# Rotary embedding on one core: 32 KB rows instead of 16 KB, and a ring of five 4 MB tiles instead of ten 2 MB ones

## The chip, the core and the metric

The kernel runs on one core of a Trainium2 chip. A core has five engines that run their own instruction streams: TensorE (PE in the profile), VectorE (DVE), ScalarE (ACT), GpSimd (POOL) and SyncE (SP), and 16 DMA engines that move data between DRAM and the on-chip memory SBUF (128 partitions). TensorE writes its results to a second memory, PSUM. Engines wait for one another, and for transfers, on semaphores. [...]the DMA engines then work through its packets. The metric is the device time of one execution in microseconds, the median of five runs.

## What is computed

The input x is 16 batches x 512 positions x 1024 float32, and each row of 1024 is 16 heads of 64 numbers. Each head's two halves are rotated by the angle of the position (the table index is the position; all heads and all batches share it):

```
x = x.reshape(batch, seq, num_heads, head_dim)
x1, x2 = x[..., :half_dim], x[..., half_dim:]
cos = cos[None, :, None, :]        # 512 x 32
sin = sin[None, :, None, :]
out = concatenate([x1 * cos - x2 * sin, x1 * sin + x2 * cos], axis=-1)
```

33.55 MB are read and 33.55 MB are written.

## The kernel before

One batch (512 rows, 2 MB) is one transfer, `c` in the code. Its 512 rows lie on 128 partitions with R = 4 neighbouring rows each, so a partition holds 16 KB that are contiguous in DRAM (`xv`, `ov`, L90 and L91). The work is done in *units* u, 64 in all: one row of every partition, 128 x 1024 numbers. `where(u)` gives the transfer, the row r in it and the place k in `x_sb`, a ring of 40 units or ten transfers (160 KB of each partition).

Since a partition holds positions 4p to 4p + 3, its part of the tables is four rows of cos and four of sin. They are loaded once into `stage` (L127) and prepared: cos in PSUM (`c_ps`, L202), minus sin beside sin for each of the four rows in SBUF by ScalarE (`s_sb`, L135 and L136) and once more in PSUM by VectorE (`s_ps`, L204 and L205).

A unit has three steps:

- x times cos into one of three PSUM tiles `t1_ps` (VectorE, `mul`, L224);
- x with the halves of each head swapped, times minus sin and sin, into one of six tiles `t2_sb`. GpSimd does this for 56 units (L193), VectorE for the 8 with u % 8 = 3, called V2 (L215);
- the sum, written over x in its place in the ring. VectorE adds 40 units (`comb`, L235). For the 24 with u % 8 in (1, 3, 6), called PE2, TensorE adds t2 to t1 in PSUM through an identity matrix (L164) and ScalarE copies the result to SBUF (L141).

VectorE's order is fixed in the program: `mul` runs two units ahead of `comb`. `mul(u)` waits for the load at the first row of a transfer, and for the PSUM tile of unit u - 3; GpSimd waits for the load and for the t2 tile of unit u - 6.

SP issues all loads in order (L124), the tables after the first one. From load 10 on it waits first until the store that holds its ring place has landed (`sem_out`). ScalarE issues the store of a transfer (L144) in its own stream, when the last unit's sum is there (`wait_added`). SP's last wait (L130) holds the program until the last ten stores have landed. Loads go through SP's queue (q1 in the profile), stores through ScalarE's (q10).

## Time and profile before

| | us |
|---|---|
| median of 5 runs | 162.05 (161.82 to 162.52) |
| the profiled execution's own time | 161.82 |
| its span in the profile | 160.4 |
| VectorE busy | 131.4 (82%) |
| GpSimd busy | 130.4 (81%) |
| TensorE busy | 80.5 (50%) |
| ScalarE busy | 26.3 (16%) |
| L193, GpSimd's product, 56 times | 2.35 each |
| L224, VectorE's product, 64 times | 1.23 each |
| L235, VectorE's sum, 40 times | 1.22 each |
| L141, ScalarE's copy, 24 times | 1.02 each |
| a load of 2 MB, issue to landing, median of 16 | 54.6 |
| a store of 2 MB, the same | 17.0 |

The span runs from the first to the last event that the profile shows; the own time of the execution is 1.4 us longer. The profile's page cuts the span in 40 slices of 4 us and gives each engine's busy share in tenths (9 is 90% or more), and for the DMA engines the mean busy share of the 16 and the GB/s that they moved. An issue is short; the time to landing holds the wait behind earlier transfers of the same queue, and the sharing with the other queue.

### The profile page before, as it was taken

To read this page: it belongs to the slowest core of one execution; us is meant where nothing else is said; L and a number is where in the kernel's file an instruction comes from. 1 tells how busy PE (TensorE), PEld (TensorE's weight loads), DVE (VectorE), ACT (ScalarE), POOL (GpSimd) and SP (SyncE) were. 2 spreads that over 40 slices of the span, in tenths; PEclk is the share of its full clock that TensorE was granted. 3 is DMA by queue.
4 is the path that set the end of the run, shared out by engine and by line. 5 is a ranking of instruction groups with operands and counts; after the bars stand their busy time and mean duration, and the time that the engine had idled before them with its cause. 6 is when DMAs were issued, how large, how long until landed. Compare 5 with 4: busy or idle time off the path is not lost.

```text
span 160.4 us, 607 instructions
## 1 busy us (share of the span) xinstructions
PE 80.5 (50%) x102; PEld 24.8 (15%) x102; DVE 131.4 (82%) x116; ACT 26.3 (16%) x27; POOL 130.4 (81%) x62
## 2 busy tenths in 40 slices
PE   6003906368535647633852853864474494475400
PEld 1002301212200211210210220112022022022000
DVE  0079299998899969999999789999999699999500
ACT  3010222021022022022112112102211202210200
POOL 1059999999999999999999993998939989399000
PEclk9999996556776556789585559585765555865555
DMA  5999999999999999999999999999999999999996
GB/s 139 402 443 429 441 425 425 417 437 437 417 449 417 437 437 415 445 421 437 423 433 437 421 441 425 433 437 421 437 429 429 441 417 441 425 429 445 417 439 282
DMA packets 4899, 67.27 MB, mean 419 GB/s; under 512 B 544, under 2 KB 800, under 8 KB 800
## 3 DMA queue, kind: packets, MB, share of 16 engines
q1 hardware_dynamic: 2592, 33.69, 49.8%
q10 hardware_dynamic: 2304, 33.56, 48.9%
q14 instruction: 3, 0.02, 0.0%
HBM read 33.69 MB, written 33.55 MB: 419 GB/s over the span
## 4 chain that ended last, share of the span: by engine, by line
POOL 42%; issue 29%; DVE 7%; PE 7%; DMA 5%; another core or an unknown queue 2%; ACT 2%; SPq 0%; POOLq 0%; DVEq 0%
POOL t_sb L193 42%; PE t_ps L164 7%; DMA stage<-in_sin_dram 5%; DVE x_sb L235 4%; DVE t_ps L224 3%; ACT x_sb L141 1%; DVE t_sb L215 1%; SPq L127 0%; SPq L124 0%; ACT s_sb L135 0%; ACT s_sb L136 0%; POOLq L116 0%; POOLq L118 0%; DVEq L223 0%
## 5 line engine op out<-in xcount | busy, mean ns | idle before, releaser
L193 POOL TENSOR_TENSOR t_sb<-x_sb,s_sb 128x1024 f32<-128x1024 f32 x56 | 129.7, 2347 | 17.5 <-DMA x_sb<-in_x_dram 9.1
L164 PE MATMUL t_ps<-t_sb,ident 128*128 128x512 f32 x96 | 77.7, 959 | 68.4 <-DVE t_ps L224 51.5
L224 DVE TENSOR_TENSOR t_ps<-x_sb,tab_ps 128x1024 f32<-128x1024 f32 x64 | 77.0, 1226 | 10.6 <-ACT x_sb L141 8.8
L235 DVE TENSOR_TENSOR x_sb<-t_ps,t_sb 128x1024 f32<-128x1024 f32 x40 | 48.6, 1217 | 0.0
L141 ACT ACTIVATE x_sb<-t_ps 128x1024 f32<-128x1024 f32 x24 | 24.6, 1023 | 117.0 <-PE t_ps L164 117.0
L164 PEld LDWEIGHTS t_ps<-t_sb,ident 128*128 128x128 f32 x96 | 24.1, 275 | 121.4 <-DVE t_ps L224 88.9
L215 DVE TENSOR_TENSOR t_sb<-x_sb,tab_ps 128x1024 f32<-128x1024 f32 x8 | 9.7, 1210 | 0.0
L202 DVE COPY tab_ps<-stage 128x128 f32<-128x128 f32 x1 | 0.3, 295 | 7.7 <-DMA stage<-in_cos_dram 7.7
L150 PE MATMUL t_ps<-zero 128*128 128x512 bf16 x6 | 2.7, 630 | 1.3 <-DVE zero L198 1.3
L135 ACT ACTIVATE s_sb<-stage 128x128 f32<-128x128 f32 x1 | 0.3, 309 | 7.0 <-DMA stage<-in_sin_dram 7.0
L135 ACT ACT_TABLE_LOAD x1 | 1.3, 1283 | 0.8 <-PEq L268 0.8
L150 PEld LDWEIGHTS t_ps<-zero 128*128 128x128 bf16 x6 | 0.7, 137 | 2.4 <-DVE zero L198 1.2
L198 DVE MEMSET zero<- 128x256 uint32 x1 | 0.3, 272 | 0.9 <-PEq L268 0.9
L175 POOL MEMSET ident<- 128x128 f32 x1 | 0.2, 204 | 0.3 <-POOLq L268 0.3
L177 POOL TENSOR_SCALAR_AFFINE_SELECT ident<-ident 128x128 f32<-128x128 f32 x1 | 0.3, 292 | 0.1
L268 POOL MEMSET const-float32-0.0<- 128x1 f32 x1 | 0.1, 98 | 0.3 <-issue 0.3
L204 DVE TENSOR_SCALAR tab_ps<-stage 128x128 f32<-128x128 f32 x1 | 0.3, 295 | 0.0
L136 ACT ACTIVATE s_sb<-stage 128x128 f32<-128x128 f32 x1 | 0.3, 293 | 0.0
L205 DVE COPY tab_ps<-stage 128x128 f32<-128x128 f32 x1 | 0.3, 284 | 0.0
L268 POOL MEMSET const-bfloat16-1.0<- 128x1 bf16 x1 | 0.1, 101 | 0.0
L268 POOL MEMSET const-uint8-127<- 128x1 uint8 x1 | 0.1, 101 | 0.0
L268 POOL MEMSET const-float32-1.0<- 128x1 f32 x1 | 0.1, 98 | 0.0
## 6 DMA issues: line engine op xcount, KB each, us to landing
x_sb<-in_x_dram SPq DMA_DIRECT2D x16, 2048.0 KB, 54.6
out_dram<-x_sb ACTq DMA_DIRECT2D x16, 2048.0 KB, 17.0
stage<-in_cos_dram SPq DMA_DIRECT2D x1, 64.0 KB, 7.7
stage<-in_sin_dram SPq DMA_DIRECT2D x1, 64.0 KB, 7.4
```

What stands on the lines that cost most here:

```text
L135: ae.activation(s_sb[:, :, 0, :], sv, COPY, scale=-1.0)
L136: ae.activation(s_sb[:, :, 1, :], sv, COPY).then_inc(sem_s, 1)
L141: ae.activation(xs[:, k, :], t1_ps[:, u % NT1, :], COPY).then_inc(sem_a, 1)
L150: pe.matmul(t1_ps[:, k, b * BANK:(b + 1) * BANK], zero[:, 0:P], zero[:], start=True, stop=True).then_inc(sem_w, 1)
L164: ins = pe.matmul(t1_ps[:, u % NT1, b * BANK:(b + 1) * BANK], ident[:], t2[:, b * BANK:(b + 1) * BANK], start=False, stop=True, skip_group ...
L177: pl.affine_select(out=ident[:], in_=ident[:], compare_op=mybir.AluOpType.is_equal, fill=0.0, base=0, pattern=[[-1, P]], channel_multiplier=1,
L193: pl.tensor_tensor(t2_sb[:, u % NT2, :, :, :], swapped(k), sin_of(s_sb, r), mult).then_inc(sem_p, 1)
L198: ve.memset(zero[:], 0.0).then_inc(sem_z, 1)
L215: ve.tensor_tensor(t2_sb[:, u % NT2, :, :, :], swapped(k), sin_of(s_ps, r), mult).then_inc(sem_d, 1)
L224: ve.tensor_tensor(t1_ps[:, u % NT1, :].rearrange("p (h d) -> p h d", d=HALF), x_sb[:, k, :, :, :].rearrange("p h t d -> p (h t) d"), c_ps ...
L235: ve.tensor_tensor(xs[:, k, :], t1_ps[:, u % NT1, :], t2_sb[:, u % NT2, :, :, :].rearrange("p h t d -> p (h t d)"), add,).then_inc(sem_v, 1)
L268: nc = _bacc.Bacc("TRN2", target_bir_lowering=False, num_devices=1)
```

## The change

A partition now holds R = 8 neighbouring rows, 32 KB that are contiguous in DRAM. 512 positions then take 64 partitions, so a tile holds two batches (BL = 2): the first on partitions 0 to 63, the second on 64 to 127 (SB = 64). There are G = 8 tiles of 4 MB. The ring stays at 40 units, which are five tiles. The load of tile 0 and the store of tile 7 are each done in two transfers of four rows of every partition (2 MB); all others are one transfer, so there are 9 loads and 9 stores. A load of tile 5 or later waits for the store of the tile five before it.

Both halves of the partitions need the same positions, so each table is loaded twice (four transfers of 64 KB), and `stage`, `c_ps` and `s_sb` hold eight rows instead of four. Since a V2 unit always has row 3 of its partition now, VectorE prepares minus sin and sin for this row alone. The units, their number, their division between engines and the order of the instructions on VectorE, GpSimd and TensorE are the same.

```diff
-    R = 4
-    assert P * R == seq
+    R = 8
+    BL = P * R // seq
+    SB = P // BL
+    G = batch // BL
...
+    def pieces(halved):
+        return [
+            (g, r, n) for g in range(G) for r, n in (((0, R // 2), (R // 2, R // 2)) if g == halved else ((0, R),))
+        ]
+    loads = pieces(0)
+    stores = pieces(G - 1)
+    load_of = [c for c, (_, _, n) in enumerate(loads) for _ in range(n)]
...
-        s_ps = tab_ps[:, R * HALF:R * (HALF + HD)].rearrange("p (r t d) -> p r t d", t=2, d=HALF)
-        xv = x.rearrange("b (p r) d -> b p (r d)", r=R)
-        ov = out.rearrange("b (p r) h d -> b p (r h d)", r=R)
+        s_ps = tab_ps[:, R * HALF:R * HALF + HD].rearrange("p (t d) -> p t d", d=HALF)
+        xv = x.rearrange("(g b) (s r) d -> g b s (r d)", b=BL, r=R)
+        ov = out.rearrange("(g b) (s r) h d -> g b s (r h d)", b=BL, r=R)
...
+        def tile(g, r, n):
+            k = (g * R + r) % RING
+            return x_sb[:, k:k + n].rearrange("p n h t d -> p (n h t d)")
+        def part(view, g, r, n):
+            return view[g, :, :, r * dim:(r + n) * dim]
...
-            for c in range(NC):
-                if c * R >= RING:
-                    sp.wait_ge(sem_out[c - RING // R], 16)
-                sp.dma_start(tile(c), xv[c]).then_inc(sem_in[c], 16)
+            for c, (g, r, n) in enumerate(loads):
+                if g * R >= RING:
+                    sp.wait_ge(sem_out[g - RING // R], 16)
+                sp.dma_start(tile(g, r, n), part(xv, g, r, n)).then_inc(sem_in[c], 16)
                 if c == 0:
                     for i, (table, sem) in enumerate(((cos, sem_cos), (sin, sem_sin))):
-                        sp.dma_start(
-                            stage[:, i, :], table.rearrange("(p r) d -> p (r d)", r=R)
-                        ).then_inc(sem, 16)
+                        for b in range(BL):
+                            sp.dma_start(
+                                stage[b * SB:(b + 1) * SB, i, :], table.rearrange("(s r) d -> s (r d)", r=R)
+                            ).then_inc(sem, 16)
...
-                if r == R - 1:
+                if u in ends:
+                    c, g, r, n = ends[u]
                     wait_added(ae, u)
-                    ae.dma_start(ov[c], tile(c)).then_inc(sem_out[c] if c < len(sem_out) else sem_rest, 16)
+                    ae.dma_start(part(ov, g, r, n), tile(g, r, n)).then_inc(
+                        sem_out[c] if c < len(sem_out) else sem_rest, 16
+                    )
...
-            sv = stage[:, 1, :].rearrange("s (r d) -> s r d", d=HALF)
-            ve.wait_ge(sem_cos, 16)
+            sv = stage[:, 1, VROW * HALF:(VROW + 1) * HALF]
+            ve.wait_ge(sem_cos, 16 * BL)
             ve.tensor_copy(c_ps, cv)
-            ve.wait_ge(sem_sin, 16)
-            ve.tensor_scalar_mul(s_ps[:, :, 0, :], sv, -1.0)
-            ve.tensor_copy(s_ps[:, :, 1, :], sv).then_inc(sem_c, 1)
+            ve.wait_ge(sem_sin, 16 * BL)
+            ve.tensor_scalar_mul(s_ps[:, 0, :], sv, -1.0)
+            ve.tensor_copy(s_ps[:, 1, :], sv).then_inc(sem_c, 1)
```

## The prediction

> **What bounds the kernel now.** I read the page's 40 slices first, then the stages, then the waits of the engines and of SP's queue, then the store issues in the timeline.

> The slices and the queues of the page:

> ```profile
> DVE  0079299998899969999999789999999699999500
> POOL 1059999999999999999999993998939989399000
> DMA  5999999999999999999999999999999999999996
> GB/s 139 402 443 429 441 425 425 417 437 437 417 449 417 437 437 415 445 421 437 423 433 437 421 441 425 433 437 421 437 429 429 441 417 441 425 429 445 417 439 282
> q1 hardware_dynamic: 2592, 33.69, 49.8%
> q10 hardware_dynamic: 2304, 33.56, 48.9%
> ```

> The 16 DMA engines are full from the first slice to the last; VectorE and GpSimd are nearly full too, but both end before the last two slices, which hold DMA alone. Loads and stores take 49.8 + 48.9 = 98.7% of the engines' span. The same by stages (busy us and count of PE, PEld, DVE, ACT, POOL; clock; DMA share; GB/s):

> ```profile
> 9.70:21.90 12.20, 5.62 (x8) 2.23 (x8) 9.27 (x9) 2.05 (x2) 12.19 (x6) 1.00 1.01 434
> 21.90:50.00 28.10, 15.48 (x20) 4.72 (x20) 26.68 (x23) 4.09 (x4) 28.10 (x13) 0.68 1.01 429
> 84.60:136.00 51.40, 28.78 (x35) 9.09 (x35) 47.80 (x42) 9.21 (x9) 44.98 (x20) 0.60 1.01 431
> 151.30:160.40 9.10, 0.00 (x0) 0.00 (x0) 0.00 (x0) 0.00 (x0) 0.00 (x0) 0.50 0.87 370
> ```

> 434 GB/s with loads alone, 429 to 431 with both directions, and 9.1 us of nothing but stores at the end. So the time is bytes over DMA rate plus two ends, as long as the store queue never runs dry once the loads are done. Whether compute threatens that, the waits and the last issues show. Who waited for whom (total us, times, longest):

> ```profile
> POOL t_sb L193 <- DMA x_sb<-in_x_dram: 9.1, 5, 2.7
> DVE t_ps L224 <- ACT x_sb L141: 8.8, 6, 2.9
> ```

> SP's own waits (total us, times, longest), for the six loads beyond the ring of ten:

> ```profile
> SPq L124 <- DMA out_dram<-x_sb: 74.5, 6, 27.3
> ```

> The last issues of stores, in ScalarE's timeline:

> ```profile
> 135.91 0.34 ACTq L144 DMA_DIRECT2D out_dram<-x_sb  x1
> ...
> 144.68 0.34 ACTq L144 DMA_DIRECT2D out_dram<-x_sb  x1
> ...
> 151.22 0.34 ACTq L144 DMA_DIRECT2D out_dram<-x_sb  x1
> ```

> GpSimd waits for loads a little; VectorE never does. The single DMA packets in the trace give the landings: load 15 at 138.8 us, stores 13, 14, 15 at 150.3, 155.2, 160.0. Store 15, issued at 151.2, had store 14 in front of it until 155.2. The chain of waits names GpSimd (42%) because it follows the last issue back; it does not show that this issue could have come some 3 us later (155.2 less 151.2 less the 1.03 us that the first load took from issue, 0.80, to first data, 1.83).

> [...]The trace has its own figure: a 512 B packet takes 27 ns, a 16,384 B one 611 ns (medians), hence 584/15,872 = 0.0368 ns per byte (27.2 GB/s an engine) and 27 - 18.8 = **8.2 ns fixed**; I use that.[...]

> **The change part by part.**

> *Rows of 32 KB.* Data packets per engine now: 32 transfers x 8 = 256 of 16 KB. After: 7 full and 2 half transfers each way, 18 x 8 = 144 (112 of 32 KB, 32 of 16 KB). 112 fewer x 8.2 ns = **-0.92 us**. Bounds: no saving if a 32 KB row is cut in two; 112 x 13 ns = -1.5 us if the excess over 0.0368 ns/B of the mean (about 616 ns) goes with the packet.

> *Semaphore packets.* 9 ns each, one per engine and transfer: 34 transfers become 18 + 4 = 22, **-0.11 us**.

> *Tables.* Each table is loaded twice, once for each half of the partitions, 1 KB rows: 4 transfers x 4 packets x (37.7 + 8.2) ns = 0.73 us per engine, against 2 x 8 x 27 ns = 0.43: **+0.30 us** of DMA. SP issues two more (0.48 us apart), covered by the 5 us that the first 2 MB take. Behind them the second half load comes 0.3 us later; nobody needs it before about 19 us.

> *Start of compute.* Tables land 0.3 us later. ScalarE's two copies go from 128x128 to 128x256: (1023 - 309)/896 = 0.8 ns an element, +0.1 each. VectorE's cos copy grows by about 0.13, its two sin copies shrink to 128x32. GpSimd starts at 9.71 + 0.3 + 0.2 = 10.2: **all compute +0.5 us**. This costs nothing while the slack at the end is larger. Each of the 64 row steps keeps its instructions, shapes and engines (1.23, 1.22, 2.35, 1.02 us), the rows multiplied on VectorE (u % 8 = 3) included: one prepared sin row now serves them all.

> *Stores of 4 MB.* The first store goes when the second did: 31.36 + 0.5 = 31.9. Until then loads fill the engines: two halves land at 8.0 and 13.8, tiles 1 and 2 at 23.5 and 33.2 (9.71 us each: 8 x 1,214 ns). In the before run the first store's data came 3.5 us after its issue; so about 36. From there both queues share, 19.4 us per tile and direction. Loads stand at 3.3 tiles at 36, the other 4.7 take 91.5: **the last lands near 128** (138.8 before, whose loads shared from 25.4). Tiles 3 to 6 land near 50, 69, 89, 108; VectorE needs tiles 3, 4, 5, 6, 7 near 65, 82, 100, 116 and 132.7. Every tile is in time, with 4 us for the last.

> *Ring of five.* Load 5 waits for store 0 (about 55) but is queued behind load 4 until 69; loads 6 and 7 wait for stores 1 and 2 (75, 94), needed at 89 and 108. SP's waits stay covered by 14 us; nothing else is queued behind them on SP. On ScalarE 9 issues take the place of 16 (0.34 us each), behind the same copies.

> *The end.* Store 6 is issued where store 13 was (135.9 + 0.5), the halves of 7 where 14 and 15 were (145.2, 151.7). With the last data at 160.04 - 0.73 = 159.3, their data have to begin at 139.8, 149.5 and 154.4; less 1.03, slack is 2.4, 3.3 and **1.7 us**. The queue doesn't run dry, and the half store keeps the same last 2 MB.

> Sum: -0.92 - 0.11 + 0.30 = **-0.73 us**: span 160.4 to 159.7, that execution's 161.82 to 161.1, and the median, 0.23 above it, 162.05 to **161.3** (-0.45%). 0.3% (0.5 us) is about what a measurement of this kernel can tell from no change.

> **The rivals.**

> *No saving* (20%): 8.2 ns rests on a 512 B load packet; if large packets hide it, or rows are cut, only +0.3 - 0.1 stays: 162.2. Against it: 16 KB packets sit at 611, not the 602 that bytes alone would take.

> *Last tile too coarse* (10%, slower): the last 4 MB tile must be whole before row 56 starts, and 8 rows of compute (17 us) follow. If loads get less than an equal share, or VectorE is late, the last issue moves past 153.4 and the engines stand idle before it. Each us beyond costs one; slower by 0.3% from 2.9 us late on (1.7 + 0.7 + 0.5), i.e. load 7 landing after about 135. At 3.5 late: 163.1. Against it: in the before run both directions moved alike, 9.75 us per 2 MB each.

> *Address pattern* (7%): [...]At 1.5% longer packets 156 x 0.015 = +2.3: 163.7.[...]

> *Few engines* (5%): [...]2 engines carry 67.1 MB at 27 GB/s each: about 1,250 us.[...]

> **How the numbers follow.** The forecast has 58%: 0.50 beyond 0.3%, 0.08 within. No saving gives 0.02 faster, 0.17 within, 0.01 slower; the coarse tile 0.02 within and 0.08 slower; pitch and engines 0.12 slower. Faster 0.52, same 0.27, slower 0.21. The forecast's own range is 160.7 (all of the 1.5 us) to 161.8; reaching to no saving and the milder coarse tile gives 160.6 to 163.1, leaving out few engines, most of pitch and the rest of the coarse tile.

> **What would show it.** Right: 2,912 packets in the two data queues in place of 4,896, 32 KB ones at 1,214 ns, the DMA row at 9 in all slices from the second to the last but one, first store issued near 32, last near 151.7, load 7 landing near 128, no long wait of VectorE for x_sb. Wrong: packets of 1,222 or more (no saving; above 1,230, pitch); a gap in the DMA row after 130 (coarse tile); a fraction of the engines busy (few engines).

## The result, and the profile after

The changed kernel takes 162.73 us (median of 28 runs, 161.63 to 163.84), the kernel before 162.02 us (49 runs, 161.76 to 162.70): a ratio of **1.0041, 95% interval 1.0027 to 1.0054**. It is slower by 0.4%; 161.3 was forecast. Besides, its times spread over 2.2 us where those of before spread over 0.9. The profiled execution took 162.39 us, its span is 161.0. Three slow runs, over 1.5% above the fastest of their kernel (two of e5, one of e8 with 173.59 us), are left out of the times, ratios and spans below.

The slices and the DMA queues of the page of the changed kernel:

```profile
DVE  0079199999899979996999969996999989997900
POOL 1049999999999999999999999799969789992000
DMA  5999999999999999999999999999999999999995
GB/s 171 389 433 505 391 407 497 399 391 489 423 391 489 423 391 432 474 391 423 482 399 423 472 407 407 480 415 407 480 415 407 480 407 415 480 407 399 436 399 216
q1 hardware_dynamic: 1616, 33.82, 49.6%
q10 hardware_dynamic: 1296, 33.56, 48.4%
q14 instruction: 2, 0.02, 0.0%
```

There are 2,912 packets in the two data queues, as forecast, and they take less: (49.6 + 48.4)% of 161.0 us is 157.8 us per engine, where (49.8 + 48.9)% of 160.4 was 158.3. These are sums of durations, and in the packet records of one engine each packet overlaps the next by 3 to 4 ns: one of 16 KB lasts 611 ns, and the next begins 607 ns after its start. 611 ns for every 607 are a share of 1.007, which is printed as 1.01, and such sums overstate what fewer packets save. The DMA row is full from the second slice to the last but one; the GB/s swing with the size of the packets (a slice of 4 us holds three). So the engines moved the data in less busy time and yet ended later. The stages that answer to those shown of before:

```profile
10.20:32.00 21.80, 11.05 (x13) 4.15 (x14) 18.20 (x17) 3.07 (x3) 21.80 (x10) 0.81 1.03 443
32.00:50.00 18.00, 11.16 (x15) 3.52 (x14) 17.12 (x15) 3.07 (x3) 18.00 (x9) 0.59 1.01 433
84.60:136.00 51.40, 31.09 (x36) 9.30 (x34) 47.17 (x41) 9.21 (x9) 46.19 (x20) 0.57 1.01 437
153.10:161.00 7.90, 0.00 (x0) 0.00 (x0) 0.00 (x0) 0.00 (x0) 0.00 (x0) 0.53 0.73 309
```

The middle reads 433 to 437 GB/s against 429 to 431. A stage's rate counts whole packets, and one packet of 32 KB on each of 16 engines is 10 GB/s of 51 us, so it can't carry a difference of 1%. The last 7.9 us, after the last issue, have a DMA share of 0.73 and 309 GB/s, against 0.87 and 370 before: in the end part of the engines have nothing left to do. The waits of GpSimd and VectorE, and those of SP:

```profile
DVE t_ps L247 <- ACT x_sb L161: 10.5, 8, 3.3
...
POOL t_sb L216 <- DMA x_sb<-in_x_dram: 1.9, 2, 1.6
```

```profile
SPq L142 <- DMA out_dram<-x_sb: 88.2, 3, 49.1
```

GpSimd's waits for loads fell from 9.1 to 1.9 us, and VectorE waits for no load: the 4 MB tiles came in time. SP waits longer, for three stores instead of six, at no cost. The last three issues of stores, in ScalarE's timeline:

```profile
138.10 0.34 ACTq L165 DMA_DIRECT2D out_dram<-x_sb  x1
...
147.08 0.34 ACTq L165 DMA_DIRECT2D out_dram<-x_sb  x1
...
153.05 0.34 ACTq L165 DMA_DIRECT2D out_dram<-x_sb  x1
```

They come 1.4 to 1.9 us later than the 136.4, 145.2 and 151.7 of the forecast. That makes a first suspect: a late last issue. A second comes out of the trace's single packets. Each engine ends a transfer with a small packet of its own (4 B, 9 ns; 352 of them for the 22 transfers), so that one can see when each of the 16 was done:

```
end of the last store, us          first engine   median   last
kernel before                          159.03     159.27   160.04
changed kernel                         158.82     158.93   160.61
```

The median engine ends 0.34 us earlier, as a saving would have it, and the last one 0.57 us later: one engine is 1.7 us behind the median, where 0.8 us was the lag before. The packets tell where it fell behind. By 70 us it lags by 0.96: a packet of 8 KB of queue 14, which the page calls `instruction` (a fetch from here on), took one engine 0.31 us at 64.4 us, and the load packet behind it took 0.66 longer than others (1,873 ns, not 1,213). By 90 us it is 1.33, by 110 us 1.73: the load packets right after its own ends of store tiles 1 and 2, at 75.1 and 94.8 us, took 0.39 us longer each. The kernel before shows the like after a fetch (0.59 at 63.4, 1,201 ns and not 611) but nothing at ends of stores.

### The profile page after: what moved, and what is told of

The parts are those of the page before. It is cut to its first block, busy times and chain, and to the rows that moved or that the text cites. A ratio compares the mean times of both kernels' runs of the same rounds, so it can differ in the third digit from the quotient of the medians.

```text
span 161.0 us, 581 instructions
## 1 busy us (share of the span) xinstructions
PE 84.8 (53%) x102; PEld 26.6 (17%) x102; DVE 131.9 (82%) x116; ACT 26.6 (16%) x27; POOL 130.6 (81%) x62
## 3 DMA queue, kind: packets, MB, share of 16 engines
q1 hardware_dynamic: 1616, 33.82, 49.6%
q10 hardware_dynamic: 1296, 33.56, 48.4%
## 4 chain that ended last, share of the span: by engine, by line
DVE 33%; PE 29%; issue 16%; ACT 9%; DMA 4%; POOL 3%; SPq 1%; DVEq 0%
PE t_ps L187 29%; DVE x_sb L258 17%; DVE t_ps L247 11%; ACT x_sb L161 8%; DVE t_sb L238 5%; DMA stage<-in_sin_dram 4%; POOL t_sb L216 3%; SPq L146 1%; ACT s_sb L154 0%; SPq L142 0%; ACT s_sb L155 0%; DVEq L246 0%; DVEq L257 0%; DVEq L244 0%
## 5 line engine op out<-in xcount | busy, mean ns | idle before, releaser
L187 PE MATMUL t_ps<-t_sb,ident 128*128 128x512 f32 x96 | 82.1, 1008 | 64.3 <-DVE t_ps L247 50.7
L247 DVE TENSOR_TENSOR t_ps<-x_sb,tab_ps 128x1024 f32<-128x1024 f32 x64 | 77.5, 1227 | 12.4 <-ACT x_sb L161 10.5
L187 PEld LDWEIGHTS t_ps<-t_sb,ident 128*128 128x128 f32 x96 | 25.8, 295 | 120.6 <-DVE t_ps L247 85.8
L161 ACT ACTIVATE x_sb<-t_ps 128x1024 f32<-128x1024 f32 x24 | 24.6, 1023 | 116.8 <-PE t_ps L187 112.0
L154 ACT ACTIVATE s_sb<-stage 128x256 f32<-128x256 f32 x1 | 0.4, 417 | 7.3 <-DMA stage<-in_sin_dram 7.3
L155 ACT ACTIVATE s_sb<-stage 128x256 f32<-128x256 f32 x1 | 0.4, 402 | 0.0
```

Source lines behind the costliest of these rows:

```text
L154: ae.activation(s_sb[:, :, 0, :], sv, COPY, scale=-1.0)
L155: ae.activation(s_sb[:, :, 1, :], sv, COPY).then_inc(sem_s, 1)
L161: ae.activation(xs[:, k, :], t1_ps[:, u % NT1, :], COPY).then_inc(sem_a, 1)
L187: ins = pe.matmul(t1_ps[:, u % NT1, b * BANK:(b + 1) * BANK], ident[:], t2[:, b * BANK:(b + 1) * BANK], start=False, stop=True, skip_group ...
L247: ve.tensor_tensor(t1_ps[:, u % NT1, :].rearrange("p (h d) -> p h d", d=HALF), x_sb[:, k, :, :, :].rearrange("p h t d -> p (h t) d"), c_ps ...
```

## The experiments

Of the three kernels that issue every store as two transfers (e2, e6, e7), most executions lost another 1.0 to 1.6 us outside the span, where the other comparable ones have 1.3 to 1.5 us there. The copy e11 issues its stores so too and has 1.3 to 1.4, so that alone isn't the reason, and it stays open; those three are compared by their spans. The mean span of the changed kernel over its executions is 161.31 us (160.2 to 162.4), that of the kernel before 160.70 (160.3 to 161.1 in 43 of its runs).

**e0, the changed kernel once more.** No edit.

> The changed kernel, unaltered, once more, for a second profile of it. Two theories of why it takes 162.7 us and not 161.3. Late compute: the last store is issued so late (153.05 us in the first profile, where 151.7 was forecast) that the DMA engines run dry in front of it; then this execution's time follows the moment of its last issue, and the last half store starts later than the first engine's end of the half store before it. Straggler: one DMA engine of the 16 falls behind the others in the course of the run (its last packet ended 1.7 us after the median engine's in the first profile, 0.8 us in that of the kernel before) and the end waits for it; then the time follows this lag, whatever the last issue does.

162.95 us, span 161.5, last issue at 152.87. No engine ran dry: the median engine ended the two half stores at 155.32 and 160.18, 4.86 us apart, the time of the data. This time the last engine is only 1.0 us behind the median, but the median itself is 1.3 us behind the first. The packets show why: after 45 us 82 load packets were longer by over 30 ns (up to 0.53 us), 1.21 us for each engine on the mean; in the first profile there were 8, and 0.15 us. Most began just behind the ends of store tiles, near 54, 74, 94 and 113 us. So the straggler looks like the small form of something that held many engines this time.

**e1, less work for VectorE.**

```diff
-                        t2_sb[:, u % NT2, :, :, :], swapped(k), over_heads(s_ps), mult
+                        t2_sb[:, u % NT2, 0:nh, :, :], swapped(k)[:, 0:nh], over_heads(s_ps)[:, 0:nh], mult
```

with `nh = H if u == VROW else 1`.

> The changed kernel with VectorE's eight sin products cut to one head of 16 from the second tile on (the rest of those rows' sin products is left out). Takes about 7 us from VectorE; DMA is untouched. Late compute: the last store is issued before 148, the engines never run dry, time about 161.2 (0.5% below the kernel before) and little spread. Straggler: last issue as early, but the time stays at 162.5 or more.

162.56 us (161.81 to 163.77), 1.0035 of the kernel before (1.0019 to 1.0050); span 161.29 on the mean, 160.4 to 162.4. The last issue in the profile:

```profile
149.00 0.34 ACTq L165 DMA_DIRECT2D out_dram<-x_sb  x1
```

Four microseconds earlier (VectorE is busy for 125.5 us instead of 131.9), and neither the mean of the span nor its spread changed. **Late compute is not the cause.**

**e2, packets of 16 KB in the changed kernel.** The same edit for loads (SP) and stores (ScalarE), waits to match:

```diff
-                sp.dma_start(tile(g, r, n), part(xv, g, r, n)).then_inc(sem_in[c], 16)
+                for h in range(r, r + n, 4):
+                    sp.dma_start(tile(g, h, 4), part(xv, g, h, 4)).then_inc(sem_in[c], 16)
```

> The changed kernel with every transfer of 4 MB issued as two of 2 MB back to back, at the same moments and behind the same waits, so that packets are 16 KB (rows of 16 KB at a pitch of 32 KB); tiles, ring, compute and issue times as in the changed kernel. Straggler (if its lag comes with the size of a packet): the lag falls to that of the kernel before, and the time to about 162.3, the 0.65 us saved on packets being lost again. Late compute: 0.65 to 0.9 us above the changed kernel, about 163.4.

163.37 us (1.0067, 1.0048 to 1.0085), but with the loss outside the span; the span is 160.81 on the mean and lies between 160.6 and 161.1. After 45 us one load packet is stretched (by 0.54 us). So the wide spread goes with packets of 32 KB. Its last issue came at 154.44, and the engines did run dry here, by 0.7 us for the median one.

**e3, finer stores at the end.**

```diff
-    stores = pieces(G - 1)
+    stores = [p for p in pieces(G - 1) if p[0] < G - 2]
+    stores += [(G - 2, 0, 4), (G - 2, 4, 4), (G - 1, 0, 4), (G - 1, 4, 2), (G - 1, 6, 2)]
```

> The changed kernel with the store of tile 6 in two halves and that of tile 7 as a half and two quarters (2, 2, 2, 1, 1 MB), each issued when its rows are done. The last issue has 1 MB behind it instead of 2, so it may come 2.4 us later before the engines run dry. Late compute: time falls to about 161.3 to 161.6. Straggler: no more than 0.2 us is won, about 162.5.

162.97 us (1.0048, 1.0034 to 1.0061), no gain, as the straggler has it. In its profile the last engine is 1.9 us behind the median, and 37 load packets are stretched after 45 us.

**e5 and e6, one direction at 16 KB.** e2's edit for the loads alone, and for the stores alone.

> The changed kernel with each load of 4 MB issued as two of 2 MB back to back (load packets of 16 KB), stores left at 32 KB. Three profiles of the changed kernel's transfers show load packets of 32 KB stretched by up to 0.7 us, most of them just after the engines pass from one store tile to the next, and hardly any stretched store packet. Stretched loads: with 16 KB load packets the stretching goes, the spread of the times narrows, and the time falls to about 162.0 (the stores' half of the 0.92 us saved stays). Any large packet: half of the loss stays, about 162.4 with the wide spread.

> The mirror of it: loads at 32 KB, each store of 4 MB issued as two of 2 MB back to back. Stretched loads: nothing is cured, about 163.0 (the changed kernel's 162.7 and 0.4 more for the stores' packets) with the wide spread. Any large packet: about 162.4. If the step from one store tile to the next is what stretches them, there is no such step less, and the stretched packets stand at the same places.

Both missed what was expected. e5: 168.93 us, 1.042 (1.039 to 1.045). e6: 164.96, 1.016 (1.0135 to 1.018); its span is 162.5 on the mean. e5's profile shows why (waits, then the last issues):

```profile
POOL t_sb L217 <- DMA x_sb<-in_x_dram: 18.8, 3, 6.7
...
DVE t_ps L248 <- DMA x_sb<-in_x_dram: 9.5, 3, 5.3
```

```profile
145.68 0.34 ACTq L166 DMA_DIRECT2D out_dram<-x_sb  x1
154.14 0.34 ACTq L166 DMA_DIRECT2D out_dram<-x_sb  x1
161.18 0.34 ACTq L166 DMA_DIRECT2D out_dram<-x_sb  x1
```

Now VectorE does wait for loads, and the last issue is 8 us late. In its packet records an engine took one packet of each queue in turn, a store packet of 1,213 ns and a load packet of 611, and the queue with the larger packets got more: between 49 and 67 us the stores moved 4 MB in 16.4 us and the loads 2 MB in 12.1, 256 against 173 GB/s. (The shares aren't 2 to 1 because the loads had the engines alone for 2.4 us between the end of one store and the first packet of the next.) In e6 it is the other way round (a 4 MB load in 14.6 us, a 2 MB store in 12.7). Equal shares, on which the forecast had built, stood where both queues had packets of one size (19.4 us for 4 MB each way in the changed kernel), and in neither of these two. For the place of the stretching these two runs decide nothing, but they show that it is not bound to load packets of 32 KB. After 45 us, 44 load packets of 16 KB were stretched in e5, by up to 0.81 us, beside stores of 32 KB, and 80 load packets of 32 KB in e6 beside stores of 16 KB; store packets were stretched in both, by up to 0.83 and 0.60 us.

**e7, 16 KB packets and less work for VectorE.** e1's and e2's edits together.

> Both loads and stores at 16 KB, as in the earlier run that gave 163.4, and VectorE's sin products cut to one head of 16 from the second tile on (the rest of them left out). That run's span was a steady 160.6 to 161.1, and its last store began 0.9 us late, having been issued at 154.4. If that gap was its only loss in the span, the span falls to about 160.2 to 160.5 here, below the kernel before or level with it; if 16 KB packets have the lag too, it stays at 160.8 or more with the wide spread.

Span 160.82 on the mean, 160.8 to 160.9 in all six (163.49 us with the loss outside it). Last issue at 148.80, no gap. So closing e2's gap won nothing, and with 16 KB packets both ways there is no wide spread. Against e1, which differs by the packets alone, the span is 0.47 us shorter although its packets have some 0.6 us more of fixed cost (112 at 5 ns, as e10 and e11 will show).

**e8 and e9, engines in step.** Both hold the fourth tile's load; e9 has e1's edit too.

```diff
+                if g == 3:
+                    sp.wait_ge(sem_m, R + 3)
                 sp.dma_start(tile(g, r, n), part(xv, g, r, n)).then_inc(sem_in[c], 16)
```

> The changed kernel, with the load of tile 3 held back on SP until VectorE has done its product of row step 10 (about 33.2 us, 1.2 us after the first store's issue at 32.0). Load 2 drains at 33.0, so the first store's packets begin on all 16 engines at once, and load 3 joins one packet later on all of them; in the changed kernel the first store joins engines that stand anywhere in their load packets. In step: if the stretched load packets come from engines that run out of step with one another (in the profile with 92 stretched packets the engines' ends of load 3 lie 1.6 us apart, in those with 14 and 17 only 0.4), the stretching goes, the span falls from a mean of 161.3 to about 160.4 with a narrow spread, the time to about 161.8. Packet size alone: stretching and spread stay, 162.7 or, with the 1 us that loads lose, up to 163.

> The same with VectorE's sin products cut to one head of 16 from the second tile on (the rest of them left out), so that a late last issue can't hide what the packets do. In step: span about 160.2 to 160.4, narrow. Packet size alone: as the earlier run with this cut and without the hold, span 161.3 on the mean, 160.4 to 162.4.

Slower: 163.37 us (1.0083, 1.0067 to 1.0099) and 163.19 (1.0074, 1.0057 to 1.0090). The spread did narrow (spans 161.7 to 162.2 and 161.6 to 162.3), but the first store's packets took about 2.1 us instead of 1.2 where the load queue had just drained, and the last issues came at 154.22 and 155.05. After 45 us e8 has 14 stretched load packets, six of them at the store ends of two engines that run late (71, 91 and 110 us); e9 has 35, 22 of them before 54 us. The hold changed two things at once, the step and the place at which the two queues meet, so it doesn't settle which one calmed the spread.

**e10 and e11, the transfers alone.** The changed kernel's loads and stores without any computation; each store waits for its load. e11 has e2's edit besides.

```diff
-                    wait_added(ae, u)
+                    ae.wait_ge(sem_in[load_of[u]], 16)
...
-        on_gpsimd(nc.gpsimd)
-        on_tensor(nc.tensor)
-        on_vector(nc.vector)
```

> The disputed packets by themselves: the changed kernel's transfers, queues and waits of SP with all computation left out; each store goes as soon as its tile has landed, so that both directions share the engines from about 14 us on. Packets of 32 KB. If the stretching is the DMA engines' own doing (32 KB packets in both directions, engines out of step), load packets are stretched here too and the times spread by 1 us or more; the span then is not 0.65 us below that of the 16 KB twin but level with it or above. If it needs the compute engines, no packet is stretched and the span lies 0.65 us below the twin's, with a narrow spread.

> The twin of it: every 4 MB transfer as two of 2 MB back to back, packets of 16 KB, again no computation. Under either reading no packet but a few is stretched and the spans lie within 0.5 us of each other; the sum of all its packets' times is 0.65 to 0.9 us larger than that of the 32 KB twin's unstretched packets.

32 KB: 161.12 us (0.9941, 0.9925 to 0.9957). 16 KB: 161.69 (0.9973, 0.9963 to 0.9984). Mean spans 159.82 and 160.37. **A saving is there: 0.55 to 0.57 us**, and after 45 us not one packet is stretched in either. But it is half of what the prediction's terms give for this pair, which differs by 112 packets and 14 semaphore packets per engine and not by the tables: 112 x 8.2 + 14 x 9 ns = 1.04 us. One stage with both directions at work, in the windows of the trace (the columns as above), of the kernel before, of the 32 KB copy and of the 16 KB copy:

```profile
40.00:127.00 87.00, 48.01 (x60) 14.44 (x60) 81.47 (x70) 15.54 (x16) 81.02 (x36) 0.67 1.01 431
```

```profile
40.00:127.00 87.00, 0.00 (x0) 1.00 1.00 434
```

```profile
40.00:127.00 87.00, 0.00 (x0) 1.00 1.01 431
```

The packet records are finer than these rates. A tile of 4 MB in and one out take 19.362 us in the 32 KB copy and 2 x 9.7245 = 19.449 in the 16 KB copy: 0.087 us less, with 16 packets and 2 semaphore packets fewer. That makes **5 ns a packet and not 8.2**, for the durations from which the 8.2 was worked out overlap: from one start to the next it is 24 ns for 512 B, 42 for 1 KB, 607 for 16 KB and 1,209 for 32 KB, and 2 x 607 - 1,209 = 5. And of e0, the changed kernel's second profile:

```profile
40.00:127.00 87.00, 52.06 (x60) 16.12 (x60) 81.03 (x70) 14.34 (x14) 83.00 (x37) 0.57 1.01 428
```

So there the stretching ate more than the saving (the first profile reads 433). What the copies lack is the computation, its instruction fetches, and the late start of the stores.

**e12, e13, e14, the paced copy.** In e12 ScalarE makes a scratch copy of 2.1 us for every row step, so that stores are issued from 25 us on, about every 18 us. e13 adds VectorE and GpSimd at work on 128 partitions of scratch, e14 adds 270 and 250 small instructions on one partition. None of the three computes the result.

```diff
             for u in range(NU):
+                if u:
+                    ae.wait_ge(sem_a, u)
+                ae.activation(flat[:, 6144:8576], flat[:, 2048:4480], COPY).then_inc(sem_a, 1)
                 if u in ends:
```

> The 32 KB copy (no computation of the result) with ScalarE held up by a copy of 2.1 us on a scratch tile for each of the 64 row steps, so that the stores are issued about every 17 us from about 27 us on, as in the changed kernel, and not as soon as a tile lands. Few instructions, little SBUF traffic. If the late start of the stores and its place among the load packets is what puts engines out of step: stretched packets and a spread of 1 us or more. If not: as the copy without it, spans 159.5 to 160.2, or longer only by a dry end, if the last issue comes after 153.

> The same with VectorE and GpSimd busy all the time on scratch tiles over 128 partitions, in 58 instructions each, so that there is SBUF traffic and hardly an instruction fetch (the result isn't computed). Traffic: load packets are stretched, span 161 or more with a spread of 1 us. Not traffic: as the paced copy.

> The paced copy with 270 and 250 small instructions on one partition on VectorE and GpSimd, each waiting for the one before it, so that there are instruction fetches in the span (queue 14 appears on the page) and hardly any SBUF traffic (the result isn't computed). Fetch: one engine falls behind by 0.6 us or more at each, its later load packets are stretched at ends of store tiles, the span rises by about 1 us and spreads. Not fetch: as the paced copy.

e12: 161.57 us (0.9959, 0.9943 to 0.9975), two stretched load packets after 45 us. In the other two my fillers outlasted the transfers (232.65 and 179.90 us), so their times say nothing; their transfers do. With SBUF traffic one load packet is stretched after 45 us, by 0.24 us, right after a fetch; the last store landed at 159.86, against 159.48 in e12. **Traffic alone did not bring it here.** With fetches (five among the transfers) four packets are stretched, and one engine ends 1.6 us behind the median, at 160.79. So fetches held up one engine, but they did not bring the stretching at the ends of store tiles. In all three, four to six engines run 1.1 us or more (up to 2.0) behind the median from the first store on, and pass their store ends unstretched: being out of step isn't enough either. All three have their stores at one place among the loads, where e12 stretches hardly anything; whether traffic or fetches add to the stretching at the place of the changed kernel was not tested.

**e15 and e16, the place at which the queues meet.** What was left is how the ends of store tiles lie to those of load tiles (median engine): 4.8 to 4.9 us after them in the first profile of the changed kernel, 3.7 to 4.6 in e0; 7.3 in the 32 KB copy, 9.9 in the paced one. e15 gives the copy a place close behind the end of a load tile, e16 gives the changed kernel one far behind it. e15: three more scratch copies ahead of e12's loop, all 2,312 elements wide instead of 2,432. e16:

```diff
-                    wait_added(ae, u)
+                    wait_added(ae, u + 1 if u == R - 1 else u)
```

> The paced copy (result not computed, ScalarE's scratch copies set the pace) with three scratch copies more ahead and all of them a little shorter, so that the stores are issued at about 32, 49, 67, 84, 101, 118, 136, 144 and 153 us, as in the changed kernel. Place: load packets are stretched at the ends of store tiles (near 54, 74, 93, 113 us), spans spread by 1 us or more, mean about 161. Computation: no packet stretched there, spans as in the other paced copy, 159.9 to 160.5 (a little more if the last issue at 153 lets the engines run dry).

> The changed kernel with one edit: ScalarE issues the first store only when the sum of row step 8 is there too, about 2.4 us later (34.4 instead of 32.0). Store tiles then end about 10 us after load tiles instead of 4.9, in the middle of a load tile. Place: few stretched packets, narrow spread, time 161.6 to 161.9, below both kernels. Computation: stretching and spread as before, about 162.7.

The first store's issue in e12 and in e15:

```profile
25.25 0.38 ACTq L162 DMA_DIRECT2D out_dram<-x_sb  x1
```

```profile
30.77 0.38 ACTq L165 DMA_DIRECT2D out_dram<-x_sb  x1
```

e15's stores went out at 30.8 us and every 17.3 us from there, store tiles ended 2.5 us after load tiles, and it took **163.75 us** (1.0116, 1.0102 to 1.0129), 2.2 us more than its twin e12, with no computation in it: 73 load packets stretched after 45 us, by up to 0.92 us, at the ends of store tiles; the last engine 2.4 us behind the median. The 16 engines end the first store tile within 0.37 us of one another, so being out of step isn't needed for it. Its times lie close together, though (163.59 to 163.93). The stage from 40 us, of e12 and of e15:

```profile
40.00:127.00 87.00, 0.00 (x0) 85.76 (x40) 0.00 (x0) 1.00 1.01 434
```

```profile
40.00:127.00 87.00, 0.00 (x0) 85.73 (x41) 0.00 (x0) 1.00 1.00 427
```

The first store's issue in the changed kernel and in e16:

```profile
31.99 0.38 ACTq L165 DMA_DIRECT2D out_dram<-x_sb  x1
```

```profile
34.31 0.38 ACTq L165 DMA_DIRECT2D out_dram<-x_sb  x1
```

e16, the changed kernel with its first store at 34.3 us instead of 32.0, took **161.91 us** (161.64 to 162.21): 0.9994 of the kernel before (0.9985 to 1.0003), 0.8 us below the changed kernel's own median, and the wide spread is gone (spans 160.2 to 160.8). Store tiles end 9.5 us after load tiles; 17 packets are stretched after 45 us, all but two of them before 60 us, and none near 75, 94 and 113. Its last store was issued at 154.31, and the engines ran dry for 0.8 us in front of it (median). Its stage:

```profile
40.00:127.00 87.00, 49.61 (x59) 15.54 (x59) 80.06 (x70) 15.35 (x15) 83.06 (x37) 0.62 1.01 434
```

A wait that only moves the first store takes the loss against the kernel before away, and scratch copies that move the place bring a loss to a copy that had none. e10 to e16 ran on one chip and e0 to e3 on another, each beside the kernel before; the changed kernel as it stands was not run beside e16, but e15 has the stretching on e16's chip. The packet records of all runs with 32 KB both ways, by place:

```
       store end after   load packets stretched    last engine behind    us, this     us, median
       load end, us      after 45 us (us/engine)   the median, us        execution    of the runs
e15        2.5              73 (1.00)                 2.4                163.78       163.75
e0         3.7 to 4.6       82 (1.21)                 1.0                162.95       -
e3         4.7              37 (0.43)                 1.9                162.90       162.97
after      4.8               8 (0.15)                 1.7                162.39       162.73
e1         4.9               5 (0.07)                 0.9                161.81       162.56
e10        7.3               0 (0.00)                 0.3                160.91       161.12
e17        7.6               4 (0.09)                 1.3                162.29       161.90
e16        9.5              17 (0.22)                 0.1                162.05       161.91
e13        9.7               1 (0.02)                 0.9                -            -
e12        9.9               2 (0.02)                 0.5                161.25       161.57
e14        9.9               4 (0.09)                 1.6                -            -
e9        13.1              35 (0.74)                 1.0                163.72       163.19
e8        14.5              14 (0.21)                 1.3                163.12       163.37
```

The counts of single executions overlap (5 packets in e1, 17 in e16), and e8 and e9 differ by their hold as well. What carries the argument are the pairs that differ by the place, over all their runs: e12 against e15, and the changed kernel against e16.

**e17, e16 with a finer end.**

```diff
-    stores = pieces(G - 1)
+    stores = [p for p in pieces(G - 1) if p[0] < G - 1]
+    stores += [(G - 1, 0, 4), (G - 1, 4, 2), (G - 1, 6, 2)]
```

> The changed kernel with the first store 2.4 us later, as before, and the second half of the last tile's store cut into two transfers of 1 MB, each issued when its two rows are done; the last issue then has 2.4 us of data behind it instead of 4.9, so the engines don't run dry. If the gap sets the end, the span falls by up to 1 us, the time to about 161.2, below both kernels by 0.4% or more. If the lagging engine sets it (in the profile it finished its first half store 0.9 us after the median engine and lost no time before the last), no more than 0.2 us is won, about 161.7 to 161.9.

161.90 us (161.58 to 162.40), **0.9988 of the kernel before (0.9978 to 0.9998)**: barely below the kernel before, by 0.12%, and level with e16 (mean spans 160.54 and 160.46). The last issue has no gap behind it any more, and the last engine is 1.3 us behind the median; the stretched load packets are those after the fetches at 61.0 and 79.3 us (0.54 and 0.22 us), one at 98.3 (0.45) and a small one at 78.8. In this profile the lagging engine sets the end; in e16's it was the gap, after which all 16 engines end within 0.2 us. So closing the gap alone wins nothing.

## Why the prediction was wrong

*What bounds the kernel*: right. e1 took 6.4 us of work from VectorE and won nothing.

*Rows of 32 KB, -0.92 us*: the step that failed, in two ways.

The smaller one is the size. The 8.2 ns rest on durations, which hold the overlap of 3 to 4 ns with the next packet; from start to start a packet saved is worth 5 ns, so 112 of them are 0.56 us. The copies show 0.55 to 0.57. The sign that the prediction named, 1,214 ns for a 32 KB packet, came true (1,213) and could not tell, since that is a duration too. With the semaphore packets at -0.07 us (6 ns each from start to start) and the tables at +0.29 (16 x 42 less 16 x 24 ns), the prediction's sum is -0.34 us and not -0.73, which is 161.7.

The greater one is that the saving was carried into the stage in which both directions share an engine, as if packets there kept their length. The measured 162.73 us lie 1.0 above even 161.7. Load packets of 32 KB were stretched there by up to 0.5 to 0.9 us each, on the mean over the engines by 0.15 us in one profile of the changed kernel and 1.21 us in another, and where the first store joins the loads decides much of it. e15 and e16 show it from both sides. e16 and e17 still lie only 0.1 to 0.2 us below the kernel before by their spans; the gap of 0.8 us in front of e16's last store and the lag of 1.3 us in e17 are at hand for the rest, but no run takes both away.

*The end as start plus the mean engine's work*: the second half of the same mistake. In the packet records a transfer's 128 packets fall to the 16 engines eight each, and no engine took over what another was late with (the lag of 1.73 us at 110 us is 1.68 at the end), so the end was that of the slowest. For the first profile: the median engine ended 0.34 us earlier than before, and its lag behind the last rose from 0.77 to 1.68, hence 0.57 us later.

*Tables, semaphore packets, start of compute*: right within 0.05 us (see above). VectorE's cos copy took 0.43 us instead of 0.29, 0.14 more where 0.13 was forecast. The summed durations of all packets fell from 158.31 to 157.68 us per engine, 0.63 with the stretching and the overlap in it; GpSimd began at 10.16 (10.2 forecast).

*Stores of 4 MB, ring of five*: right. First store issued at 31.99 (31.9), load 7 landed at 129.1 (near 128), no tile late. The equal shares behind it came with packets of one size in both queues; with two sizes, in e5, they were 256 and 173 GB/s.

*The end*: the last issue came 1.4 us later than forecast. VectorE waited 10.5 us for ScalarE instead of 8.8, at a mean clock of TensorE of 0.659 instead of 0.685; this is read off the profiles and no run isolates it. The slack took it up: e1 shows that it cost nothing.

*The rivals.* The coarse last tile fell with e1 and e3. Few engines, an assumption of the author's that no trace of the kernel before bore on, fell with the first page (a DMA row of 9, the mean of 16 engines). No saving fell with the copies, though a fixed cost of 5 ns puts the truth between it and the forecast. The address pattern came nearest in what it would show, longer packets; but its 1.5% was the author's assumption, not worked out from a trace, and its reason, the wider pitch of the rows, isn't what decides: e12 and e15 have the same pitch, packets and transfers, and differ by 2.2 us. What it should have been is a rival on the two streams' places to each other; the prediction had none.

## What to carry to other kernels

Transfers bound this kernel, and larger packets saved a fixed cost that was small (5 ns a packet, 0.55 us in the copies), while stretched packets cost more than that (1.21 us an engine in e0). Price a packet from start to start, not by its duration, if the records overlap. Where loads and stores share the engines, look at when the first store joins, and try a wait that moves it by an eighth of a tile: here that was worth 0.8 us, more than the packets were. Keep the packets of both queues of one size: with 32 KB one way and 16 KB the other, e5 took 4.2% longer than the kernel before, and e6's span was 1.1% longer.
